# A decoder trunk on one core: six prepared pieces and three parts in the last stage, with more of its products in sevens

## The chip, the core and the metric

The kernel runs on one core of a Trainium2 chip. The metric is the device time of one execution, in microseconds (us). Five engines matter. TensorE (PE) multiplies and transposes, and its weight loads are shown as a row of their own (PEld). VectorE (DVE) does element-wise work. ScalarE (ACT) does casts, copies and functions. GpSimd (POOL) does very little here, and SyncE (SP) issues all DMAs.

## The reference

The reference is a trunk of two layers on 256 tokens of width 2048, all in f32. Each layer has a token mixer (retention in layer 0, a gated short convolution in layer 1) and then a SwiGLU feed-forward part of width 5632. Each half of a layer is normed, scaled and shifted by vectors that come from a conditioning vector, and its result is gated before it is added to the residual. A norm closes the trunk. What the change touches is the feed-forward part of layer 1:

```
h = rms_norm(x, norm2_g[1]) * (1.0 + sc2) + sh2
a, b = jnp.split(h @ ffn_w_in[1], 2, axis=-1)      # (256, 2048) @ (2048, 2 * 5632)
x = x + g2 * ((silu(a) * b) @ ffn_w_out[1])        # (256, 5632) @ (5632, 2048)
return rms_norm(x, final_g)
```

## The kernel before, in words

**Precision in three products.** An f32 matrix is held as two parts, `hi` (the value rounded to the matmul's input type) and `lo` (what is left). A product of two such matrices is three matmuls, hi x hi, hi x lo and lo x hi, added up in a PSUM bank (`thrice`, lines 457 to 462). Weights come from HBM as f32 and are split on the core.

**How weights are prepared.** All weights lie in one array `w_all` in the order of their use, cut into raws of 128 x 2048 (1 MB). `fetch` (line 370) loads one into one of three raw buffers. `prepare` (lines 376 to 406) makes one piece of it: ACT casts it to `hi` (L402), then DVE subtracts to get `lo` (L405). Pieces of 128 x 1024 lie in four places (`PART_BUFS`), each a pair of `hi` and `lo`. `take` (line 410) hands the pieces to PE in order and calls `prepare` so that `ahead_now` pieces beyond the one in use are asked for: two in most of the kernel, three in the last stage (line 1394). A piece's place is free again when PE has read it.

**The order of work.** PE's order is the program's, written out by hand. On DVE and ACT the tile framework's scheduler decides at build time which instruction comes when, by the program's order and given priorities; at run time each engine goes through its queue in that order, and waits on semaphores.

**The last stage.** The feed-forward part of layer 1 works on 44 tiles of 128 of the inner width, in two parts of 20 and 24 tiles (`LAST_TILES`). Four tiles of the first part are made in another way first, while the norm is still being computed (`first_rows`, line 1373). The rest go in *input groups* of four tiles (`last_input`, line 1313): 512 columns of `a` and 512 of `b`, for two halves of 128 tokens each, so four PSUM banks of 128 x 512, summed over the 16 tiles of the width 2048. There are four such groups in the first part and six in the second. After each, DVE and ACT make silu(a) * b, and PE turns the result (eight transposes, L1331), before the third pair of rows in the next group; ACT and DVE then split it into the tiles of `mid`. When a part's input is done, two *output groups* of 1024 columns each (`last_output`, line 1342) multiply its `mid` tiles with the second matrix and add the gated result to the residual `xt` (`gated`, lines 1205 and 1206).

**Pairs and sevens.** The sum of a group runs over pairs of row tiles. With two row tiles, two column blocks of 512 and two halves of tokens, an ordinary pair is eight block products, 24 matmuls of 512 columns, and two pieces of prepared weights. A `Seven` (line 142) does the same by the Strassen-Winograd scheme with seven block products (`sevens`, line 1224): 21 matmuls. It needs sums and differences. Those of the weights are made in `prepare`: DVE makes the differences of 128 x 1024 (L391) and two sums of 128 x 512 (L395, L397), and there are four pieces to split (2, 3, 4 and 5), three of 128 x 1024 and one of 128 x 512. Those of the tokens are made by `tokens_sums_of` (line 1139), for the input once per pair (`made_in_sums`, line 1158), for the output once per pair and part (line 1338). Four of a seven's products go into four extra PSUM banks, and after the last seven of a group `mixed_sums` (line 1237) combines these with one copy on ACT and four operations on DVE, so that with the group's own four banks all eight are in use; DVE adds the plain sums later (L1317, L1365).

`IN_SEVEN` names the pairs done as sevens in an input group (of eight pairs), `OUT_SEVEN` those in the output groups of each part. Which four-wide order the first part's output pairs are taken in is set in `last_out` (line 178), since the last input group's tiles are turned only two pairs into the output. At the end of the last output group, six row tiles are taken column by column, so that one half of the tokens can be finished and stored while PE works on the other (`stored`, line 1249).

Of the kernel before, what the change touches and what calls it, by code (L numbers as in the profile page):

```python
# [17 lines left out]
P = 128  # L18
# [19 lines left out]
LEAD = 6  # L38
ROOTS_AT, SPREAD_AT = 1, 3
TAIL_ROWS = 6  # L40
IN_SEVEN, OUT_SEVEN, TURNS_AT, BESIDE_CB, BESIDE_SUMS = (3, 4, 6), ((2, 4, 6), (2, 4, 6)), 2, 40, 48
LAST_TILES = 20, 24
STORE_AT, LOAD_AT = 0, 2
LEAD_RET, LEAD_CONV, LEAD_FFN = 6, 4, 2
AHEAD = 2
# [2 lines left out]
MOD_PRIO = -300  # L48
STEPS = (8, 8, 20)
RAW_BUFS = 3  # L50
PART_BUFS = 4
LEFT, ENDS, EARLIER = 8, 2, 120

Q0, K0, V0, G0 = 0, HEADS * DK, 2 * HEADS * DK, 2 * HEADS * DK + HEADS * DV
# [112 lines left out]
def last_in():  # L167

    n, rows = LAST_TILES[0], [(i, [2 * i, 2 * i + 1]) for i in range(KT // 2)]
    cols = [part * DFF + j * P for j in range(n - 4, n) for part in range(2)]
    firsts = [Group(cols[:LEAD])] + [Group([c]) for c in cols[LEAD:]]
    fours = [[*range(0, n - 4, 4)], [*range(n, FT, 4)]]
    return firsts, [[in_pairs([j * P, DFF + j * P], rows, IN_SEVEN) for j in js] for js in fours]


def last_out(part):

    first, n = part * LAST_TILES[0], LAST_TILES[part]  # L180
    order = list(range(n // 2))
    if not part:
        a, b = order[-2:]
        order = order[:5] + [a, order[6], b, order[5], order[7]]
    rows = [(i, [first + 2 * i, first + 2 * i + 1]) for i in order]
    out = []
    for c in range(0, D, 2 * DV):
        cols, rest = [c, c + DV], 0
        if part and c + 2 * DV == D:
            rest = TAIL_ROWS // 2  # L190
        out.append(in_pairs(cols, rows[: len(rows) - rest], OUT_SEVEN[part]))
        if rest:
            out[-1] += [Group([col], DV, ks=[k for _, r in rows[-rest:] for k in r]) for col in cols]
    return out


LAST_FIRSTS, LAST_IN = last_in()
LAST_OUT = [last_out(part) for part in range(2)]


def in_use_order():

    for g in RET_SPANS:
        yield "ret_w_in", 0, g
    for n, h in enumerate(HEAD_ORDER):
        qkg, v = RET_HEADS[h]
        for g in qkg[:2] + [v] + qkg[2:]:
            yield "ret_w_in", 0, g
        if n % (HEADS // 2) == HEADS // 2 - 1:
            for g in RET_OUT[n // (HEADS // 2)]:  # L210
                yield "ret_w_out", 0, g
    for layer in range(DEPTH):
        if layer == 1:
            for g in CONV_IN:
                yield "conv_w_in", 0, g
            for g in CONV_OUT:
                yield "conv_w_out", 0, g
        for part in range(2):
            ins, outs = FFN_IN[part], FFN_OUT[part]
            if layer == DEPTH - 1:  # L220
                ins, outs = sum(LAST_IN[part], [] if part else LAST_FIRSTS), sum(LAST_OUT[part], [])
# [35 lines left out]
def trunk(ctx: ExitStack, tc: tile.TileContext, x_in, c_in, pos_in, w_mod, cols_in, gain_in, tab_in, w_all, out):  # L257
# [8 lines left out]
    def name(s):  # L266
        serial[0] += 1
        return f"{s}_{serial[0]}"
# [107 lines left out]
    def prepare(between=None):  # L376
        if prepared[0] == len(pieces):
            return
        _, piece = pieces[prepared[0]]
        prepared[0] += 1  # L380
        if piece in (0, 2):
            if not fetched:
                fetch()
            raws[:] = [fetched.pop(0)]
            while first <= units[0] < early and len(fetched) < RAW_BUFS - 1 and n_fetched[0] < w_all.shape[0]:
                fetch()
        whole = raws[0]
        b = [whole[:, i : i + DV] for i in range(0, CHUNK, DV)]
        raw = whole[:, :HALF] if piece in (0, 4) else whole[:, HALF:]
        if piece == 2:  # L390
            nc.vector.tensor_tensor(differences, whole[:, DV : 3 * DV], whole[:, : 2 * DV], op=ALU.subtract)  # L391
        elif piece == 3:
            raw = differences
        elif piece == 4:
            nc.vector.tensor_tensor(b[1], b[2], differences[:, :DV], op=ALU.subtract)  # L395
        elif piece == 5:
            nc.vector.tensor_tensor(b[3], b[3], b[1], op=ALU.subtract)  # L397
            raw = b[3]
        width = raw.shape[1]
        hi = wpool.tile([P, HALF], F32R, tag="hi", name=name("hi"))[:, :width]  # L400
        lo = wpool.tile([P, HALF], F32R, tag="lo", name=name("lo"))[:, :width]
        nc.scalar.copy(hi, raw)  # L402
        if between:
            between()
        nc.vector.tensor_tensor(lo, raw, hi.bitcast(F32), op=ALU.subtract)  # L405
        ready.append((hi, lo, width))

    prepared, ahead_now = [0], [AHEAD]

    def take(group, k, col, width=P):  # L410

# [778 lines left out]
    def spread():  # L1190
        whole = gate_row.rearrange("a b -> (a b)").unsqueeze(0)
        for i in range(2):
            o = slice(i * D // 2, (i + 1) * D // 2)
            nc.sync.dma_start(flat[i], whole[:, o].broadcast_to([P, D // 2]))
    total = mpool.tile([P, 2, 4], F32, tag="total", name="total")
    sums_of = mpool.tile([P, 2], F32, tag="sums", name="sums")

    def flat_bank():
        return bank().rearrange("p a b -> p (a b)")
# [69 lines left out]
    def gathered(groups, act, base, sums, beside=None, mixed=None):  # L1269

        ours = {(t, j): flat_bank() for t in range(2) for j in range(2)}
        banks, n = [], len(sums)
        for i, g in enumerate(groups):
            if beside:
                beside(i)
            if i == TURNS_AT and waiting:
                waiting.pop(0)()
            if isinstance(g, Seven):
                n -= 1
                banks = banks or [flat_bank() for _ in range(4)]  # L1280
                of = sums[(g.ks[0] - base) // 2]
                sevens(g, act, base, of, ours, banks, n == len(sums) - 1, n == 0)
                if not n:
                    extra = mixed_sums(banks)
                    if mixed:
                        mixed(extra)
                continue
            if len(g.cols) == 1:
                tail = TAIL_ROWS if g is groups[-1] else 0
                late, j = [], g.cols[0] // DV % 2  # L1290
                for k in g.ks:
                    weights = take(g, k, *g.items[0])
                    rows = (act[k - base], False, k == g.ks[-1])
                    if tail:
                        late.append((*weights, *rows))
                    else:
                        by_token([ours[t, j] for t in range(2)], *weights, *rows)
                    paced(g.n)
                for t in range(2):
                    for args in late:  # L1300
                        by_token([ours[t, j] for t in range(2)], *args, halves=[t])
                    added(t, g.cols[0] // DV, ours[t, j], True)
                    if tail:
                        stored(t)
                continue
            for k in g.ks:
                for j, item in enumerate(g.items):
# [33 lines left out]

    def last_output(part, c, groups, act, base):

        final = part and c

        def beside(i):
            if not part and not c and i == STORE_AT:
                gate_stored()
            if not part and not c and i == LOAD_AT:
                spread()  # L1350
            if part and not c and i == LOAD_AT:
# [13 lines left out]
            nc.vector.tensor_tensor(extra[t, j], pt, extra[t, j], op=ALU.add)  # L1365
        for (t, j), v in extra.items():
            gated(t, c + j, v, MOD_PRIO)
            if part:
# [16 lines left out]
            for turn_of in turns[4 * (i - 1) : 4 * i] if i else ():  # L1385
                turn_of()

    for part in range(2):
        n = LAST_TILES[part] // 2
        mid = mids(LAST_TILES[part]) if part else first_mid  # L1390
        if not part:
            first_rows(mid[-2:])
            made_in_sums()
            ahead_now[0] = AHEAD + 1
        for i, groups in enumerate(LAST_IN[part]):
            due = OUT_SEVEN[part]
            seven = [tokens_sums[due.index(q)] if q in due else None for q in (2 * i, 2 * i + 1)]
            last_input(groups, mid[2 * i : 2 * i + 2], seven)
        act = [mid[k // 2][:, k % 2] for k in range(2 * n)]
        for c, groups in enumerate(LAST_OUT[part]):  # L1400
            last_output(part, 2 * c, groups, act, part * LAST_TILES[0])
    assert not todo


# [34 lines left out]
```

## Time and profile before

| what | value |
|---|---|
| runs, us | 2594.22, 2595.54, 2592.18; median 2594.22 |
| profiled execution, us | 2593.25 |
| its span, us | 2591.5 |
| mean granted TensorE clock | 0.998 |
| DVE busy over the span | 2197.4 us, 85% |
| HBM traffic | 689.56 MB, mean 266 GB/s |

The page of a profile gives each engine's busy time as a share of the span. A view by stretches gives the same for any window, and the number of instructions in it after an x. A view by line groups instructions: line, engine, operation, output and input tiles with their shapes and count, then the busy time and the mean duration in ns of one, then the engine's idle time just before them and what ended it. The timeline has one row per instruction, or per run of equal ones: start, duration, engine, line, tiles, count, and in brackets the idle time before it. The view of waits has the waiting engine and tile, what it waited for, and the total in us, the count and the longest. Matmuls are pipelined, so their shown durations overlap, and what one costs is read from the distance between starts.

### The profile page before, as it was taken

The page shows a single profiled execution, that of the slowest core. Times are in us where ns is not written, and L with a number is a line of the kernel's source. Part 1 is how long each engine was busy: PE and PEld are TensorE (multiplying, and loading weights), DVE is VectorE, ACT ScalarE, POOL GpSimd, SP SyncE. Part 2 cuts the span into 40 slices and gives each one's busy share as a digit, 9 for nine tenths or more (in the row PEclk, how much of TensorE's full clock was granted, in tenths as well). Part 3 has the DMA queues.
Part 4 walks back from the last instruction along what each step waited for, and adds up shares of the span by engine and source line. Part 5 has one row for each costly group of instructions (what it writes and reads, how often), then busy time and mean ns, then how long its engine had stood idle before and what let it go on. Part 6 is the DMA issues. An engine that isn't in the chain of part 4 may idle for free.

```text
span 2591.5 us, 36408 instructions
## 1 busy us (share of the span) xinstructions
PE 2563.3 (99%) x14181; PEld 2236.3 (86%) x14181; DVE 2197.4 (85%) x2762; ACT 1306.0 (50%) x1792; POOL 125.9 (5%) x232
## 2 busy tenths in 40 slices
PE   7999999999999999999999999999999999999998
PEld 6898889888889888888888898888998888888887
DVE  7988978787698887777778889988989998999978
ACT  5544543444456545334444454444565554556554
POOL 0000000110000000100001001000000000000001
PEclk9999999999999999999999999999999999999999
DMA  9975768767676888777877768877845565555654
GB/s 398 388 293 209 268 243 306 300 248 277 251 282 246 330 323 307 301 296 298 298 294 283 298 237 313 330 297 277 308 165 210 188 223 205 180 210 187 222 208 147
DMA packets 96688, 689.56 MB, mean 266 GB/s; under 512 B 10737, under 2 KB 12161, under 8 KB 13441
## 3 DMA queue, kind: packets, MB, share of 16 engines
q1 hardware_dynamic: 96514, 687.23, 71.3%
q8 instruction: 111, 1.82, 0.3%
q14 instruction: 63, 0.52, 0.1%
HBM read 685.08 MB, written 2.11 MB: 265 GB/s over the span
## 4 chain that ended last, share of the span: by engine, by line
PE 94%; DVE 3%; DMA 2%; issue 1%; ACT 1%; ACTq 0%; POOLq 0%; POOL 0%; DVEq 0%
PE bank L447 30%; PE bank L450 16%; PE bank L461 12%; PE bank L460 12%; PE bank L462 12%; PE bank L495 2%; PE bank L496 2%; PE bank L494 2%; PE bank L627 1%; PE bank L629 1%; PE bank L628 1%; DVE raw L755 1%; DMA raw<-w_all 1%; DVE lo L405 1%; PE bank L983 1%
## 5 line engine op out<-in xcount | busy, mean ns | idle before, releaser
L402 ACT CAST hi<-raw 128x1024 fp32r<-128x1024 f32 (+1 forms) x954 | 978.9, 1033 | 1015.8 <-PE bank L447 346.4
L405 DVE TENSOR_TENSOR lo<-raw,hi 128x1024 fp32r<-128x1024 f32 (+1 forms) x954 | 1133.9, 1197 | 322.6 <-ACT hi L402 317.3
L447 PE MATMUL bank<-h,hi 128*128 128x512 f32 x2016 | 699.3, 390 | 0.0
L450 PE MATMUL bank<-h,lo 128*128 128x256 f32 x2016 | 568.5, 282 | 0.0
L447 PEld LDWEIGHTS bank<-h,hi 128*128 128x128 f32 x2016 | 378.4, 188 | 79.2
L460 PE MATMUL bank<-hi,h 128*128 128x512 f32 x1032 | 405.0, 392 | 2.2 <-DVE rm L739 2.2
L461 PE MATMUL bank<-lo,h 128*128 128x512 f32 x1032 | 404.3, 392 | 0.0
L462 PE MATMUL bank<-hi,h 128*128 128x512 f32 x1032 | 402.7, 390 | 0.0
L450 PEld LDWEIGHTS bank<-h,lo 128*128 128x128 f32 x2016 | 381.0, 189 | 0.1
L318 DVE SCALAR_TENSOR_TENSOR raw<-raw,cb 128x2048 f32<-128x2048 f32 x160 | 365.5, 2284 | 15.7 <-DMA raw<-w_mod 15.3
L447 PE MATMUL bank<-mid,hi 128*128 128x512 f32 x922 | 319.8, 390 | 0.0
L450 PE MATMUL bank<-mid,lo 128*128 128x256 f32 x922 | 260.1, 282 | 0.4 <-DVE lo L405 0.4
L460 PEld LDWEIGHTS bank<-hi,h 128*128 128x128 f32 x1032 | 194.4, 188 | 40.7 <-DVE rm L739 2.8
L462 PEld LDWEIGHTS bank<-hi,h 128*128 128x128 f32 x1032 | 194.2, 188 | 40.8
L461 PEld LDWEIGHTS bank<-lo,h 128*128 128x128 f32 x1032 | 194.5, 188 | 40.4 <-DVE lo L405 3.3
L447 PEld LDWEIGHTS bank<-mid,hi 128*128 128x128 f32 x922 | 173.1, 188 | 36.2
L450 PEld LDWEIGHTS bank<-mid,lo 128*128 128x128 f32 x922 | 174.2, 189 | 0.7 <-DVE lo L405 0.7
L447 PE MATMUL bank<-rm,hi 128*128 128x512 f32 x496 | 172.5, 390 | 0.0
L496 PE MATMUL bank<-h,lo 128*128 128x256 f32 x512 | 146.4, 286 | 4.6 <-DVE lo L405 4.6
L494 PE MATMUL bank<-h,hi 128*128 128x256 f32 x512 | 146.1, 285 | 3.4 <-ACT h L783 3.4
L495 PE MATMUL bank<-h,hi 128*128 128x256 f32 x512 | 146.1, 285 | 0.7 <-DVE h L784 0.7
L450 PE MATMUL bank<-rm,lo 128*128 128x256 f32 x496 | 139.8, 282 | 0.0
(256 smaller groups left out, 3197.4 us busy)
## 6 DMA issues: line engine op xcount, KB each, us to landing
raw<-w_all SPq DMA_DIRECT2D x456, 1024.0 KB, 4.8
raw<-w_mod SPq DMA_DIRECT2D x192, 1024.0 KB, 5.2
x<-x_in SPq DMA_DIRECT2D x4, 512.0 KB, 5.3
out<-xt SPq DMA_DIRECT2D x4, 512.0 KB, 3.0
decay<-tab_in SPq DMA_DIRECT2D x8, 128.0 KB, 2.4
x<-gate_row SPq DMA_DIRECT2D x2, 512.0 KB, 4.8
last_gain<-gain_in SPq DMA_DIRECT2D x1, 1024.0 KB, 7.2
cols<-cols_in SPq DMA_DIRECT2D x1, 152.0 KB, 8.3
```

Of the source, the lines that this page charges most:

```text
L318: nc.vector.scalar_tensor_tensor(raw, raw, 1.0, cb, op0=ALU.mult, op1=ALU.mult, accum_out=total)
L402: nc.scalar.copy(hi, raw)
L405: nc.vector.tensor_tensor(lo, raw, hi.bitcast(F32), op=ALU.subtract)
L447: nc.tensor.matmul(pt, hi, h, start=fresh and k == g.ks[0], stop=False, skip_group_check=True)
L450: nc.tensor.matmul(pt[:, 1, :], lo, h[:, 0, :], start=False, stop=last and k == g.ks[-1], skip_group_check=True)
L460: nc.tensor.matmul(o, hi, w_hi, start=first, stop=False)
L461: nc.tensor.matmul(o, hi, w_lo, start=False, stop=False)
L462: nc.tensor.matmul(o, lo, w_hi, start=False, stop=last)
L494: nc.tensor.matmul(pt, hi, h[:, 0, :], start=first, stop=False, skip_group_check=True)
L495: nc.tensor.matmul(pt, hi, h[:, 1, :], start=False, stop=False, skip_group_check=True)
L496: nc.tensor.matmul(pt, lo, h[:, 0, :], start=False, stop=last, skip_group_check=True)
L627: nc.tensor.matmul(pt, hi, high, start=k == 0, stop=False, skip_group_check=True)
```

## The change

- The last stage goes in three parts of 12, 16 and 16 tiles instead of two of 20 and 24. There are still ten input groups (two, four and four), but six output groups instead of four.
- Four of the eight pairs of each input group are sevens (3, 4, 5, 6 instead of 3, 4, 6). In the output, two pairs of six are sevens in the first part and three of eight in each of the others; before, three of ten and three of twelve.
- In the last stage two more places for prepared pieces lie in the pool `last`, used by turns with the four of before, and five pieces beyond the one in use are asked for instead of three.
- The two small tiles `total` and `sums_of` move to another pool, and a spacing tile gets smaller.
- `gathered` counts a group's sevens from the group itself.

```diff
-IN_SEVEN, OUT_SEVEN, TURNS_AT, BESIDE_CB, BESIDE_SUMS = (3, 4, 6), ((2, 4, 6), (2, 4, 6)), 2, 40, 48
-LAST_TILES = 20, 24
+IN_SEVEN, OUT_SEVEN, TURNS_AT, BESIDE_CB, BESIDE_SUMS = (3, 4, 5, 6), ((1, 2), (3, 4, 6), (2, 3, 4)), 2, 40, 32
+LAST_TILES = 12, 16, 16
...
-PART_BUFS = 4
+PART_BUFS, MORE_BUFS = 4, 2
...
-    first, n = part * LAST_TILES[0], LAST_TILES[part]
-    order = list(range(n // 2))
+    first = sum(LAST_TILES[:part])
+    order = list(range(LAST_TILES[part] // 2))
     if not part:
-        a, b = order[-2:]
-        order = order[:5] + [a, order[6], b, order[5], order[7]]
+        n = len(order) - 5
+        order = order[:n] + order[-2:] + order[n:-2]
...
-        if part and c + 2 * DV == D:
+        if part == len(LAST_TILES) - 1 and c + 2 * DV == D:
...
-        hi = wpool.tile([P, HALF], F32R, tag="hi", name=name("hi"))[:, :width]
-        lo = wpool.tile([P, HALF], F32R, tag="lo", name=name("lo"))[:, :width]
+        pool, bufs = wpool, PART_BUFS
+        if last_pool and prepared[0] % (PART_BUFS + MORE_BUFS) < MORE_BUFS:
+            pool, bufs = last_pool[0], MORE_BUFS
+        hi = pool.tile([P, HALF], F32R, tag="hi", name=name("hi"), bufs=bufs)[:, :width]
+        lo = pool.tile([P, HALF], F32R, tag="lo", name=name("lo"), bufs=bufs)[:, :width]
...
-    total = mpool.tile([P, 2, 4], F32, tag="total", name="total")
-    sums_of = mpool.tile([P, 2], F32, tag="sums", name="sums")
+    total = work.tile([P, 2, 4], F32, tag="total", name="total", bufs=1)
+    sums_of = work.tile([P, 2], F32, tag="sums", name="sums", bufs=1)
...
-    for part in range(2):
-        n = LAST_TILES[part] // 2
-        mid = mids(LAST_TILES[part]) if part else first_mid
+    for part, tiles in enumerate(LAST_TILES):
+        mid = mids(tiles) if part else first_mid
         if not part:
             first_rows(mid[-2:])
             made_in_sums()
-            ahead_now[0] = AHEAD + 1
+            last_pool.append(mpool)
+            ahead_now[0] = AHEAD + 1 + MORE_BUFS
```

More of the change, by code (lines that the diff above doesn't have):

```diff
@@ L173, in last_in @@
     firsts = [Group(cols[:LEAD])] + [Group([c]) for c in cols[LEAD:]]
-    fours = [[*range(0, n - 4, 4)], [*range(n, FT, 4)]]
+    fours = [[*range(0, n - 4, 4)]]
+    for m in LAST_TILES[1:]:
+        fours.append([*range(n, n + m, 4)])
+        n += m
     return firsts, [[in_pairs([j * P, DFF + j * P], rows, IN_SEVEN) for j in js] for js in fours]
 def last_out(part):
-    first, n = part * LAST_TILES[0], LAST_TILES[part]
-    order = list(range(n // 2))
+    first = sum(LAST_TILES[:part])
+    order = list(range(LAST_TILES[part] // 2))
     if not part:
-        a, b = order[-2:]
-        order = order[:5] + [a, order[6], b, order[5], order[7]]
+        n = len(order) - 5
+        order = order[:n] + order[-2:] + order[n:-2]
     rows = [(i, [first + 2 * i, first + 2 * i + 1]) for i in order]
@@ L197 @@
 LAST_FIRSTS, LAST_IN = last_in()
-LAST_OUT = [last_out(part) for part in range(2)]
+LAST_OUT = [last_out(part) for part in range(len(LAST_TILES))]
 def in_use_order():
@@ L217, in in_use_order @@
                 yield "conv_w_out", 0, g
-        for part in range(2):
-            ins, outs = FFN_IN[part], FFN_OUT[part]
-            if layer == DEPTH - 1:
-                ins, outs = sum(LAST_IN[part], [] if part else LAST_FIRSTS), sum(LAST_OUT[part], [])
+        parts = list(zip(FFN_IN, FFN_OUT))
+        if layer == DEPTH - 1:
+            parts = [(sum(ins, [] if i else LAST_FIRSTS), sum(outs, [])) for i, (ins, outs) in enumerate(zip(LAST_IN, LAST_OUT))]
+        for ins, outs in parts:
             for g in ins:
@@ L406, in prepare @@
         ready.append((hi, lo, width))
-    prepared, ahead_now = [0], [AHEAD]
+    prepared, ahead_now, last_pool = [0], [AHEAD], []
     def take(group, k, col, width=P):
@@ L1271, in gathered @@
         ours = {(t, j): flat_bank() for t in range(2) for j in range(2)}
-        banks, n = [], len(sums)
+        banks, n = [], sum(isinstance(g, Seven) for g in groups)
+        left = n
         for i, g in enumerate(groups):
@@ L1278, in gathered @@
             if isinstance(g, Seven):
-                n -= 1
+                left -= 1
                 banks = banks or [flat_bank() for _ in range(4)]
                 of = sums[(g.ks[0] - base) // 2]
-                sevens(g, act, base, of, ours, banks, n == len(sums) - 1, n == 0)
-                if not n:
+                sevens(g, act, base, of, ours, banks, left == n - 1, left == 0)
+                if not left:
                     extra = mixed_sums(banks)
@@ L1342, in last_output @@
     def last_output(part, c, groups, act, base):
-        final = part and c
+        last = part == len(LAST_TILES) - 1
+        final = last and c
         def beside(i):
@@ L1350, in beside @@
                 spread()
-            if part and not c and i == LOAD_AT:
+            if last and not c and i == LOAD_AT:
                 last_gain = hpool.tile([P, D], F32, tag="h", name="last_gain")
@@ L1367, in last_output @@
             gated(t, c + j, v, MOD_PRIO)
-            if part:
+            if last:
                 xs, n = at(xt[t], c + j), c + j
@@ L1386, in first_rows @@
                 turn_of()
-    for part in range(2):
-        n = LAST_TILES[part] // 2
-        mid = mids(LAST_TILES[part]) if part else first_mid
+    for part, tiles in enumerate(LAST_TILES):
+        mid = mids(tiles) if part else first_mid
         if not part:
@@ L1398, in trunk @@
             last_input(groups, mid[2 * i : 2 * i + 2], seven)
-        act = [mid[k // 2][:, k % 2] for k in range(2 * n)]
+        act = [mid[k // 2][:, k % 2] for k in range(tiles)]
         for c, groups in enumerate(LAST_OUT[part]):
-            last_output(part, 2 * c, groups, act, part * LAST_TILES[0])
+            last_output(part, 2 * c, groups, act, sum(LAST_TILES[:part]))
     assert not todo
```

## The prediction

> **What bounds the kernel now.** I read the page first, then the table of stretches for the last stage alone, then the timelines of TensorE (PE) and VectorE (DVE) in it, then the waits, then the groups by line with shapes kept apart.
>
> ```profile
> span 2591.5 us, 36408 instructions
> ...
> PE 2563.3 (99%) x14181; PEld 2236.3 (86%) x14181; DVE 2197.4 (85%) x2762; ACT 1306.0 (50%) x1792; POOL 125.9 (5%) x232
> ```
>
> The page says only that PE is always busy and that DVE is second. The change touches one stage, so the share that counts is that stage's. It runs from the first product of the first paired group (1923.8) to the last matmul (2582.4):
>
> ```profile
> core 0: us, PE busy (x) PEld busy (x) DVE busy (x) ACT busy (x) POOL busy (x), PEclk, DMA share, GB/s
> 1923.80:2582.40 658.60, 658.06 (x2934) 542.18 (x2932) 593.70 (x712) 366.70 (x433) 7.46 (x7) 1.00 0.55 195
> 2574.10:2582.40 8.30, 8.30 (x38) 6.67 (x36) 5.96 (x11) 2.79 (x8) 2.08 (x5) 1.00 0.00 0
> 2311.30:2353.90 42.60, 42.60 (x192) 35.09 (x191) 39.98 (x51) 25.34 (x31) 0.00 (x0) 1.00 0.55 198
> ```
>
> In this stage DVE is busy 593.7 of 658.6 us, 90%: 64.9 us are free. In one input group (the last row) it is 39.98 of 42.60, so 2.6 us are free. ACT (366.7) and the DMA engines (0.55) have room.
>
> Is PE at its peak, or only shown as busy? Its timeline gives the pitch:
>
> ```profile
> 1923.82 0.48 PE L460 MATMUL bank<-hi,h 128*128 128x512 f32 x1
> ...
> 1940.26 0.39 PE L460 MATMUL bank<-hi,sum 128*128 128x512 f32 x1
> ...
> 1949.78 0.39 PE L460 MATMUL bank<-hi,h 128*128 128x512 f32 x1
> ...
> 1992.39 0.39 PE L460 MATMUL bank<-hi,h 128*128 128x512 f32 x1
> ...
> 2035.00 0.39 PE L460 MATMUL bank<-hi,h 128*128 128x512 f32 x1
> ...
> 2582.17 0.39 PE L462 MATMUL bank<-hi,mid 128*128 128x512 f32 x1
> ```
>
> Two sevens, 42 matmuls, lie between 1940.26 and 1949.78: 9.52 / 42 = 0.2267 us each. An ordinary pair is 24 matmuls, 5.44 us; a seven is 21, 4.76 us. A whole input group takes 2035.00 - 1992.39 = 42.61 us; five pairs and three sevens are 183 matmuls, 41.48 us, and the eight transposes take the other 1.13. Over the stage, ten input groups (1830 matmuls), the output of the first part (2 x (10 x 24 - 9) = 462) and of the second (2 x (12 x 24 - 9) = 558) are 2850 matmuls, 646.1 us; with 11.3 of transposes 657.4, against 658.6. So PE sets the stage, and all its waiting comes to little over 1 us.
>
> The waits of the stage show how DVE and ACT stand to it:
>
> ```profile
> ACT hi L402 <- PE bank L462: 215.6, 224, 1.9
> DVE lo L405 <- ACT hi L402: 57.1, 80, 1.5
> ...
> PEld bank L461 <- DVE lo L405: 4.6, 12, 1.0
> ```
>
> ACT waits for PE to free a prepared piece's place, and DVE waits for ACT: preparation is ahead, held by the four places. PE's weight loads waited for DVE only 4.6 us, most of it hidden.
>
> **The change, part by part.** *PE.* Sevens in the input matrix go from 10 groups x 3 = 30 to 10 x 4 = 40 (still ten groups: 2 + 4 + 4). In the output matrix they go from 2 x (3 + 3) = 12 to 2 x (2 + 3 + 3) = 16. That is 14 more, each three matmuls less: 14 x 3 x 0.2267 = 9.5 us. Transposes stay at 80. PE would need 658.6 - 9.5 = 649.1 us.
>
> *DVE.* These rows carry its prices; first the groups, then their pitch where they run back to back:
>
> ```profile
> L405 DVE TENSOR_TENSOR lo<-raw,hi 128x1024 fp32r<-128x1024 f32 x245 | 296.4, 1220 | 52.3 <-ACT hi L402 49.3
> ...
> L391 DVE TENSOR_TENSOR x<-raw 128x1024 f32<-128x1024 f32 x42 | 51.1, 1217 | 0.3 <-DMA raw<-w_all 0.3
> L397 DVE TENSOR_TENSOR raw<-raw 128x512 f32<-128x512 f32 x42 | 29.0, 690 | 1.0
> L405 DVE TENSOR_TENSOR lo<-raw,hi 128x512 fp32r<-128x512 f32 x42 | 28.8, 686 | 6.7 <-ACT hi L402 6.5
> L395 DVE TENSOR_TENSOR raw<-raw,x 128x512 f32<-128x512 f32 x42 | 28.7, 683 | 0.0
> ...
> L1168 DVE TENSOR_TENSOR u<-h 128x256 f32<-128x256 f32 x4 | 1.7, 418 | 0.0
> ```
>
> ```profile
> 2327.74 0.68 DVE L1317 TENSOR_TENSOR x<-bank,x 128x512 f32<-128x512 f32 x1
> 2328.34 0.68 DVE L1317 TENSOR_TENSOR u<-bank,u 128x512 f32<-128x512 f32 x1
> ...
> 2342.09 0.28 DVE L512 TENSOR_TENSOR mid<-u,mid 128x128 fp32r<-128x128 f32 x1
> 2342.29 0.28 DVE L1146 TENSOR_TENSOR u<-u,u 128x128 f32<-128x128 f32 x1
> ...
> 2343.63 0.55 DVE L512 TENSOR_TENSOR in_cb<-u,in_cb 128x384 fp32r<-128x384 f32 x1
> 2344.10 1.82 DVE L405 TENSOR_TENSOR lo<-raw,hi 128x1024 fp32r<-128x1024 f32 x2
> ...
> 2352.69 3.49 DVE L405 TENSOR_TENSOR lo<-raw,hi 128x1024 fp32r<-128x1024 f32 x3
> 2356.10 1.22 DVE L405 TENSOR_TENSOR lo<-x,hi 128x1024 fp32r<-128x1024 f32 x1
> 2357.23 0.68 DVE L395 TENSOR_TENSOR raw<-raw,x 128x512 f32<-128x512 f32 x1
> 2357.95 0.69 DVE L397 TENSOR_TENSOR raw<-raw 128x512 f32<-128x512 f32 x1
> ```
>
> A 1024-wide operation lasts 1.22 us, but three in a row take 3.49: (3.49 - 1.22) / 2 = 1.135 from start to start. A 512-wide one starts 0.60 after the last (2327.74 to 2328.34), or 0.72 behind one whose result it needs (L395 to L397). A 128-wide one takes 0.20, the 384-wide one 0.47. So the next instruction starts 0.085 us before the one ahead has ended, and each gap that closes frees 0.085 more than the idle time shows.
>
> An ordinary pair costs DVE two 1024-wide `lo`: 2.27 us. A seven costs one difference and three `lo` of 1024 (4.54), one `lo` of 512 (0.60), and L395 and L397 (1.32): 6.46. So a seven gives PE 0.68 us and takes 4.19 from DVE; fourteen take 58.7. The third part brings two more output groups, each with the four sums of the mixed products, four additions of the plain ones and eight operations with gate and residual: 2 x 16 x 0.60 = 19.2. Two more output pairs need sums of tokens (five 128-wide and one 384-wide, 1.47): 2.9. One more input pair needs them (two of 256 at 0.42 from L1168's mean, eight of 0.20): 2.4. Sum: 83.2 us.
>
> One price is weighed here. The Trainium skill (VectorE: DVE Perf Modes, section "Side-by-side: where the cycles go") gives an instruction its elements plus 8 and some 150 cycles at 0.96 GHz, which would be about 1.23 us for 1024 and 0.70 for 512; as an estimate, the 28 wide and 74 half-wide instructions added would then cost 34.5 + 51.7, with the small ones about 92 us, and the forecast would be some 15 us later. The trace agrees with 1.22 as a duration, but the 3.49 for three shows that the next one does not wait for it, so the pitch stands.
>
> *What DVE has for it.* 64.9 us idle and 80 x 0.085 = 6.8 from the gaps (the 80 waits above): 71.7. The need is 83.2. Even with no idle moment DVE is 83.2 - 71.7 = 11.5 us short, so DVE becomes the bound and PE's 9.5 us are lost in waiting. By one input group the same: DVE's 39.98, less 0.4 for five gaps, plus 4.19 is 43.8 us, against PE's 42.61 - 0.68 = 41.93.
>
> *Idle time that stays.* In the last 8.30 us DVE is idle for 2.3: the weights are all prepared and the end hangs on the last products. That stays: 13.8. Inside, an input group now has 2.34 us of gaps (2.6 less rounding at its edges); over ten groups 23.4. All stand behind casts that waited for a place, so six places should close most; but four sevens run one after the other now (pairs 3 to 6), each a chain of DVE, ACT and DVE again. Bounds for what stays: nothing and 23.4. I take 6, a quarter, since the waits above name PE's places for 215.6 us. Sum: 13.8 + 6 = 19.8.
>
> *Edits at nothing.* Six places instead of four fit in what four tiles less of `mid` leave, and hold at most two pieces more ahead: once, at the start, 2 x 1.135 = 2.3 us, only in the low bound, since DVE is not idle there. `total` and the sums only change their pool. ACT gets 14 x 1.5 casts of about 1 us, 21 on 366.7, and stays the third engine. The weights are the same megabytes in the same loads. Sums of tokens for pair 2 of the first part are needed two pairs after their transposes (10.2 us) instead of four: about 3 us of DVE work, covered unless DVE is behind, and then it is in the sum already.
>
> The profiled run took 2593.25 us, 1.75 more than its span; 2593.25 + 19.8 = 2613.1. The median of the runs shown is 0.97 above the profiled one: **2614**.
>
> **The rivals.** *DVE keeps up, faster.* If the gaps are only want of places, six places close them, PE never waits, and the gain is the whole 9.5: 2594.2 - 9.5 = 2584.7. It decides where DVE's work in an input group falls below 41.93 us; for it speaks that every gap is behind a place, against it 43.8. The Trainium skill (Perfetto Trace Analysis, section "Optimization Strategy") says that the same gap repeated can mean too few buffers; the trace agrees with the 215.6 us of ACT behind PE's places, and by that rule the outcome is this rival's.
>
> *About the same.* DVE's work is dearer than PE's saving, but some prices are lower than the pitch says; 83.2 would have to be 65, a fifth less, for 2594 to 2596.
>
> *Much slower: the chains stay.* The two further places do not help (held by pieces that wait for each other, or DVE's order puts a wait for PE's bank ahead of the piece that PE wants): all 23.4 of gaps remain. 13.8 + 23.4 = 37.2: 2631.4. For it speaks the line of four sevens, 19.0 us of PE against 25.8 of DVE; against it that today's casts wait for PE rather than for DVE. It would also be the time if the places did not come into use at all.
>
> **How the numbers follow.** Forecast 0.65, the chains stay 0.20, DVE keeps up 0.08, the same 0.07. Own range of the forecast: 11.5 (the tail's 2.3 met by the lead) to 13.8 + 16, so 2605.7 to 2624. The range reaches up to the chains, 2632, and down by 5% of DVE's sum (4.2), to 2601. A measurement of this kernel can tell about 0.2%, 5.2 us, from no change. Faster by over that: 0.08; within: 0.07; slower: 0.85.
>
> **What would show it.** Right: in the last stage PE's matmul count falls by 42 but the stage is some 20 us longer; DVE is busy about 98% there; the waits of PE's weight loads on DVE `lo` grow from 4.6 to 20 us or more, mostly in pairs 3 to 6 of the input groups; ACT's waits for PE's places shrink from 215.6 to well under half. An input group takes about 44 us rather than 42.61. Wrong: input groups of 41.9 us with PE at its pitch throughout (DVE's prices or my count are off), or DVE idle as now while PE waits (the chains).

## The result, and the profile after

The changed kernel takes 2623.14 us (median of 4, 2621.87 to 2624.13), the kernel before beside it 2593.20 (median of 4): 1.0117 times as long, 95% interval 1.0105 to 1.013, or 29.9 us. The forecast was 2614 and slower, with a range from 2601 to 2632. The granted clock was the same in both (0.998 and 0.997), so it has no part in this. Lines of the changed file stand three to eight lower: the cast to `hi` is L408, the subtraction for `lo` L411, the difference L394, and the sums L398 and L400.

The page of the changed kernel, to be read against that of before:

```profile
span 2622.3 us, 36476 instructions
## 1 busy us (share of the span) xinstructions
PE 2563.2 (98%) x14139; PEld 2228.5 (85%) x14139; DVE 2273.2 (87%) x2886; ACT 1321.7 (50%) x1832; POOL 121.3 (5%) x232
...
PE 75%; DVE 17%; DMA 3%; issue 3%; ACT 2%; POOL 0%; ACTq 0%; DVEq 0%; SPq 0%
```

PE has 42 matmuls less, as counted, and is shown busy as long as before: a busy PE here is a PE that holds an instruction. The last line, the chain that ended last, tells more. Before, DVE had 3% of it, and now it has 17%; the line of before:

```profile
PE 94%; DVE 3%; DMA 2%; issue 1%; ACT 1%; ACTq 0%; POOLq 0%; POOL 0%; DVEq 0%
```

The table of stretches cuts the last stage at the first product with `mid` and the first one with `h`, so its rows are in turn the input and the output groups of each part; the last row is what lies behind the last matmul. The kernel before first, then the changed one:

```profile
1923.82:2093.46 169.64, 169.64 (x760) 139.57 (x759) 157.20 (x202) 99.91 (x125) 0.00 (x0) 1.00 0.55 193
2093.46:2200.06 106.60, 106.06 (x472) 87.55 (x471) 91.66 (x107) 55.61 (x62) 0.00 (x0) 1.00 0.59 212
2200.06:2454.79 254.73, 254.73 (x1140) 209.75 (x1138) 236.35 (x279) 146.02 (x167) 0.00 (x0) 1.00 0.55 196
2454.79:2582.40 127.61, 127.61 (x567) 105.29 (x565) 108.46 (x127) 65.14 (x79) 7.46 (x7) 1.00 0.51 181
2582.40:2591.50 9.10, 0.16 (x1) 0.00 (x0) 3.08 (x6) 2.67 (x5) 0.55 (x1) 0.68 0.58 230
```

```profile
1924.17:2013.33 89.16, 84.41 (x373) 68.03 (x371) 87.64 (x129) 52.85 (x76) 0.00 (x0) 1.00 0.48 177
2013.33:2076.97 63.64, 63.64 (x286) 52.52 (x284) 62.43 (x77) 36.57 (x44) 0.00 (x0) 1.00 0.64 233
2076.97:2258.30 181.33, 170.95 (x745) 138.06 (x745) 174.78 (x212) 99.22 (x117) 0.00 (x0) 0.99 0.49 179
2258.30:2342.17 83.87, 83.87 (x375) 69.52 (x374) 80.65 (x96) 47.89 (x55) 0.00 (x0) 1.00 0.58 215
2342.17:2520.26 178.09, 170.04 (x746) 136.62 (x744) 174.31 (x215) 100.06 (x120) 0.00 (x0) 1.00 0.50 183
2520.26:2608.38 88.12, 85.18 (x375) 69.02 (x373) 86.69 (x106) 43.91 (x57) 1.77 (x3) 1.00 0.45 168
2608.38:2622.30 13.92, 0.16 (x1) 0.00 (x0) 5.73 (x12) 4.51 (x10) 2.18 (x5) 0.67 0.38 151
```

The ten input groups took 169.64 + 254.73 = 424.4 us and now take 89.16 + 181.33 + 178.09 = 448.6, though PE's own work in them is 6.8 us less. The output groups took 234.2 and now take 235.6. So of the 30.8 us by which the span grew, 24.2 came in the input groups, 1.4 in the output, 4.8 behind the last matmul (9.1 before, 13.9 now), and 0.35 lies ahead of the stage. DVE, the third busy figure of a row, fills every input row to 96% or more.

The waits of the stage in the changed kernel:

```profile
ACT hi L408 <- PE bank L468: 110.1, 75, 4.7
ACT hi L408 <- DVE raw L398: 59.0, 32, 4.0
ACT hi L408 <- DVE x L394: 48.1, 21, 3.5
ACT hi L408 <- DMA raw<-w_all: 38.4, 31, 3.1
PEld bank L467 <- DVE lo L411: 26.8, 25, 1.8
PE bank L467 <- DVE lo L411: 17.3, 19, 1.3
DVE lo L411 <- ACT hi L408: 13.5, 24, 1.6
...
PEld bank L466 <- DVE x L1250: 6.1, 3, 3.5
PE bank L466 <- DVE x L1250: 4.8, 3, 3.1
```

DVE's wait for ACT's casts has gone from 57.1 to 13.5 us, and ACT now waits for DVE (59.0 and 48.1, were 33.2 and 4.5) about as much as for PE's places (110.1, was 215.6). PE's weight loads wait for `lo`, 26.8 us where it was 4.6. The order of who waits for whom has turned round. One wait is new: ACT's casts wait 38.4 us for the loads of raw weights, for which they did not wait before. The raw buffers are still three, and in both kernels the DMA queue waits for DVE's subtraction (L405, now L411) ahead of 119 of the stage's loads.

### The profile page after: what moved, and what is told of

The parts are those of the page before. It is cut to its first block, busy times and chain, and to the rows that moved or that the text cites. A ratio compares the mean times of both kernels' runs of the same rounds, so it can differ in the third digit from the quotient of the medians.

```text
span 2622.3 us, 36476 instructions
## 1 busy us (share of the span) xinstructions
PE 2563.2 (98%) x14139; PEld 2228.5 (85%) x14139; DVE 2273.2 (87%) x2886; ACT 1321.7 (50%) x1832; POOL 121.3 (5%) x232
## 4 chain that ended last, share of the span: by engine, by line
PE 75%; DVE 17%; DMA 3%; issue 3%; ACT 2%; POOL 0%; ACTq 0%; DVEq 0%; SPq 0%
PE bank L453 28%; PE bank L456 15%; DVE lo L411 8%; PE bank L467 7%; PE bank L468 7%; PE bank L466 7%; DMA raw<-w_all 3%; PE bank L502 2%; PE bank L501 2%; PE bank L500 2%; DVE x L394 2%; PE bank L633 1%; PE bank L635 1%; PE bank L634 1%; ACT hi L408 1%
## 5 line engine op out<-in xcount | busy, mean ns | idle before, releaser
L408 ACT CAST hi<-raw 128x1024 fp32r<-128x1024 f32 (+1 forms) x968 | 975.2, 1026 | 957.5 <-PE bank L453 296.7
L411 DVE TENSOR_TENSOR lo<-raw,hi 128x1024 fp32r<-128x1024 f32 (+1 forms) x968 | 1137.9, 1192 | 267.5 <-ACT hi L408 264.0
L467 PE MATMUL bank<-lo,h 128*128 128x512 f32 x992 | 390.4, 394 | 15.3 <-DVE lo L411 15.2
L466 PE MATMUL bank<-hi,h 128*128 128x512 f32 x992 | 391.5, 395 | 9.9 <-DVE x L1250 4.8
L468 PE MATMUL bank<-hi,h 128*128 128x512 f32 x992 | 387.8, 391 | 0.0
L467 PEld LDWEIGHTS bank<-lo,h 128*128 128x128 f32 x992 | 187.4, 189 | 57.5 <-DVE lo L411 22.6
L466 PEld LDWEIGHTS bank<-hi,h 128*128 128x128 f32 x992 | 187.2, 189 | 51.7 <-DVE x L1250 6.1
L468 PEld LDWEIGHTS bank<-hi,h 128*128 128x128 f32 x992 | 187.1, 189 | 39.0
```

The source lines that it names most:

```text
L466: nc.tensor.matmul(o, hi, w_hi, start=first, stop=False)
L467: nc.tensor.matmul(o, hi, w_lo, start=False, stop=False)
L468: nc.tensor.matmul(o, lo, w_hi, start=False, stop=last)
```

## The experiments

Three theories were tested. *Work*: VectorE's sum of work sets the stage, either over the whole stage or within each input group. *Row of sevens*: the chain from DVE to ACT and back in four sevens one after the other stalls, and places would bridge it. *Parts*: the third part and its end cost the time. Each ratio below is to the kernel before, timed beside it on the same chip; the chips differ from one experiment to another, so two experiments are compared best by their ratios. Where a diff changes one name of a line that sets several, only that name is shown.

**Three parts, old sevens in the input.**

```diff
-IN_SEVEN = (3, 4, 5, 6)
+IN_SEVEN = (3, 4, 6)
```

> Three parts and six places as changed, output sevens as changed, but three sevens per input group as before. Theory of work (VectorE's sum of work sets the last stage): VectorE gets 4 more sevens x 4.19 + two output groups 19.2 + sums of tokens 2.9 = 38.9 us more, under the 71.7 us it has free; TensorE needs 4 x 0.68 = 2.7 us less, so 2588 to 2596. Rival of the parts (the third part's two output groups and its end are what costs): over 2605. Rival of the row of sevens (four in a row stall the chain): as the theory of work, since no four stand in a row.

2591.35 us, 0.9995 (0.9985 to 1.0004): no change. The third part, its two output groups, four more output sevens and six places cost nothing together. So with six places the ten additional input sevens cost 2623 - 2591 = 32 us, and the rival of the parts falls as it was put (over 2605). With four places both come out differently, as a run below shows.

**Two parts, four sevens in the input.** This is the same addition by itself, on the kernel before.

```diff
-IN_SEVEN = (3, 4, 6)
+IN_SEVEN = (3, 4, 5, 6)
```

> The kernel before with four sevens per input group (pairs 3 to 6) and nothing else: two parts, four places. Theory of work taken over the whole stage: 10 x 4.19 + 2.4 = 44.3 us of VectorE's 71.7, TensorE 6.8 less, 2586 to 2594. Theory of work taken group by group (43.8 us of VectorE per input group, which the output groups can't make good): 10 x 1.2 longer, about 2605. Rival of the row of sevens: over 2612.

2607.10 us, 1.0052 (1.0037 to 1.0067). The stage, cut into input and output groups of each part as above:

```profile
1921.04:2097.70 176.66, 172.98 (x748) 135.78 (x746) 173.48 (x231) 107.07 (x137) 0.00 (x0) 1.00 0.50 185
2097.70:2203.45 105.75, 105.75 (x472) 87.63 (x471) 92.06 (x108) 55.70 (x63) 0.00 (x0) 1.00 0.59 213
2203.45:2468.10 264.65, 259.62 (x1122) 204.06 (x1120) 258.08 (x308) 155.72 (x180) 0.00 (x0) 1.00 0.51 189
2468.10:2595.72 127.62, 127.62 (x567) 105.32 (x565) 108.84 (x128) 64.71 (x79) 7.48 (x7) 1.00 0.49 181
```

DVE is idle for 42.2 us of 674.7, and still the stage is 16 us longer than the 658.6 of before. Of this idle time 9.8 us lie in the input groups and 32.5 in the output groups, where the additional work isn't: the account holds group by group, not over the whole stage. The expected 2605 of that reading was met to 2 us.

**Four places.**

```diff
-PART_BUFS, MORE_BUFS = 4, 2
+PART_BUFS, MORE_BUFS = 4, 0
```

> The changed kernel with four places and three pieces asked for ahead, as before. Theory of work: VectorE is short of time whatever it has in store, so within some 12 us of the changed kernel, 2618 to 2635. Rival of the row of sevens (the chain from VectorE to ScalarE and back is what stalls, and places are what bridges it): over 2640.

2618.20 us, 1.0095 (1.008 to 1.011). Where DVE is short of time, the two places bring nothing; the kernel is rather 5 us faster without them. That speaks against the row of sevens. One moment of the changed kernel shows a price of running far ahead. At 2384.84 the second input group of the third part begins, and PE needs banks that DVE is still to free with the merging of the group before (L1249 to L1252). DVE, then PE, then ACT:

```profile
2383.33 1.23 DVE L411 TENSOR_TENSOR lo<-raw,hi 128x1024 fp32r<-128x1024 f32 x1 [0.43 <-ACT hi L408]
2384.48 0.68 DVE L1249 TENSOR_TENSOR u<-bank,x 128x512 f32<-128x512 f32 x1
...
2386.21 0.68 DVE L1250 TENSOR_TENSOR x<-bank,u 128x512 f32<-128x512 f32 x1
...
2388.54 0.68 DVE L1252 TENSOR_TENSOR u<-bank,u 128x512 f32<-128x512 f32 x1
```

```profile
2386.95 0.50 PE L466 MATMUL bank<-hi,h 128*128 128x512 f32 x1 [0.58 <-DVE x L1250]
...
2389.28 0.50 PE L466 MATMUL bank<-hi,h 128*128 128x512 f32 x1 [1.37 <-DVE u L1252]
```

```profile
2382.25 1.05 ACT L408 CAST hi<-raw 128x1024 fp32r<-128x1024 f32 x1 [3.09 <-DMA raw<-w_all]
2383.21 0.58 ACT L1248 COPY x<-bank 128x512 f32<-128x512 f32 x1
```

The copy that begins the merging (L1248) stands in ACT's queue behind a cast for a later piece, and that cast waited 3.09 us for its load. The merging on DVE comes behind the `lo` of that same piece, with two more `lo` in between. Over the whole stage PE's matmuls wait 8.7 us behind DVE's operations on banks with six places and 1.4 with four. In return its weight loads wait less for `lo` (26.8 against 42.8). The two stages are nearly equal, 684.2 and 682.9. Of the 6.2 us between the two profiled spans, 1.4 lie in the stage, 2.3 behind the last matmul, and 2.5 ahead of the stage, where the edit changes nothing: the stage begins between 1921.0 and 1925.9 us in the runs of this document. So in this pair 3.7 us fall where the places are in use.

**Three parts, old sevens, four places.**

```diff
-IN_SEVEN = (3, 4, 5, 6)
+IN_SEVEN = (3, 4, 6)
-PART_BUFS, MORE_BUFS = 4, 2
+PART_BUFS, MORE_BUFS = 4, 0
```

> Three parts and three sevens per input group as in the run of that name, but four places instead of six. If the two places are worth something only where VectorE has time to get ahead, TensorE's weight loads wait 5 to 8 us more in the last stage than with six, and the whole takes 2595 to 2600. If the places are worth nothing anywhere, as between the changed kernel and the same with four, 2590 to 2593.

2601.58 us, 1.0034 (1.0022 to 1.0046), against 0.9995 with six. Here the two places are worth 10 us: DVE has time to get ahead, and PE's weight loads wait 11.8 us for `lo` with four places and 1.0 with six. So the places pay where DVE has time in sum and lacks it only in a burst. The time is a little over the 2595 to 2600 that was expected.

Read with the runs above, this one also shows that no part of the change has a price of its own. With four places the third part and its output sevens cost 9 us (2601.58 against 2592.55 beside it), which six places give back. With four places the ten additional input sevens cost 2618.20 - 2601.58 = 16.6 us, about as in two parts (15.3), and not 32. What the kernels with three parts and four input sevens have in common is a stage of 683 to 684 us, with four places or six. What the places shorten is the stage with three: 663.1 us with four, 653.5 with six.

**The difference on GpSimd.**

```diff
-nc.vector.tensor_tensor(differences, whole[:, DV : 3 * DV], whole[:, : 2 * DV], op=ALU.subtract)
+nc.gpsimd.tensor_tensor(differences, whole[:, DV : 3 * DV], whole[:, : 2 * DV], op=ALU.subtract)
```

> The changed kernel with the differences of 128 x 1024 that a seven needs made on GpSimd instead of VectorE. Theory of work: 56 x 1.135 = 63.6 us leave VectorE, 83.2 - 63.6 = 19.6 of its 71.7 us are needed, TensorE sets the stage again: 2584 to 2595. Rival of the row of sevens: the chain gets longer by a slower engine, so 2623 or over.

2662.15 us, 1.0268 (1.025 to 1.0285): far outside the range of the theory of work, and inside that of its rival. The work left DVE, but two things came back. The changed kernel's groups on DVE first, then this kernel's, and its GpSimd group:

```profile
L400 DVE TENSOR_TENSOR raw<-raw 128x512 f32<-128x512 f32 x56 | 38.8, 692 | 1.0
L398 DVE TENSOR_TENSOR raw<-raw,x 128x512 f32<-128x512 f32 x56 | 38.7, 691 | 0.0
...
L1324 DVE TENSOR_TENSOR x<-bank,x 128x512 f32<-128x512 f32 x20 | 13.7, 685 | 0.8 <-PE bank L468 0.8
```

```profile
L400 DVE TENSOR_TENSOR raw<-raw 128x512 f32<-128x512 f32 x56 | 62.5, 1116 | 0.6
...
L398 DVE TENSOR_TENSOR raw<-raw,x 128x512 f32<-128x512 f32 x56 | 38.3, 683 | 43.7 <-POOL x L394 43.7
L1329 DVE TENSOR_TENSOR x<-x,u 128x512 f32<-128x512 f32 x20 | 21.5, 1082 | 0.7 <-ACT x L1328 0.7
L1324 DVE TENSOR_TENSOR x<-bank,x 128x512 f32<-128x512 f32 x20 | 13.6, 682 | 0.0
```

```profile
L394 POOL TENSOR_TENSOR x<-raw 128x1024 f32<-128x1024 f32 x56 | 174.8, 3121 | 568.2 <-DMA raw<-w_all 275.7 <-DVE lo L411 165.9 <-DVE raw L398 67.4
```

A difference takes 3.12 us on GpSimd, and DVE stands still for 43.7 us behind it. And DVE's own operations get longer: L400 goes from 692 to 1116 ns on average, with nothing changed in it. The average hides two kinds: 45 of the 56 stay at about 0.69 us, and 11 are longer, up to 2.89. The Trainium skill (SBUF — State Buffer, section "SBUF: two separate sides") says that a pair of ports is shared by GpSimd and a VectorE operation with two SBUF inputs, and that whichever starts first holds it for the whole instruction. The trace agrees. L400 reads two SBUF tiles: its 11 longer ones all began after a difference on GpSimd had begun and ended 0.55 us behind it, and 17 others that began before the difference beside them stayed short. L1324 reads a PSUM bank, lies beside a difference 25 times of 40 and stays at 0.68 us. L398 reads two SBUF tiles too and stays at 0.68, but it waits for GpSimd's result and so never runs beside it.

DVE is busy for 666.7 us of the stage, as in the changed kernel, and idle for 60.2. So the run exchanged one shortage of DVE for another and added a wait for a slower engine, which is what the rival said of this run. It decides nothing between the two theories. A cleaner way to take the work away follows.

**Without the difference.** The same subtraction is left out, so that the sevens compute with a tile that isn't theirs; all else stays.

```diff
-nc.vector.tensor_tensor(differences, whole[:, DV : 3 * DV], whole[:, : 2 * DV], op=ALU.subtract)
+pass
```

> The changed kernel without the subtraction that makes a seven's difference of 128 x 1024; the tile keeps what lay in it, so the sevens compute with other numbers. Everything else, matmuls, casts, places and order, stays. Theory of work: 56 x 1.135 = 63.6 us leave VectorE, which has more than enough time then; TensorE sets the stage at some 649 us and the whole takes 2582 to 2590. Group by group the same, 43.8 - 4.5 = 39.3 us against 41.93. Rival of the row of sevens (ScalarE's and VectorE's chain through the casts, not the sum of work): over 2605.

2582.78 us, 0.9959 (0.9945 to 0.9973):

```profile
1923.93:2569.97 646.04, 646.04 (x2892) 535.24 (x2890) 608.42 (x777) 382.52 (x468) 1.80 (x4) 1.00 0.54 199
```

With the matmuls, casts, parts and places of the changed kernel and 56 VectorE instructions less, PE runs the stage in 646.0 us, 12.5 less than before, and no row of four sevens stalls anything. PE's 9.5 us were there to be had; DVE's work took them. The other 3 us came from small waits of the kernel before: what the starts of its matmuls lie apart beyond 0.2267 us adds up to 3.7 us in the stage, in pieces of about 0.1 that the view of waits leaves out, and to 1.2 here. One reservation: the run takes away a link of the chain as well as work, since ACT's cast of a difference no longer waits for it (48.1 us in the changed kernel). By itself it doesn't tell the two apart.

**The same work without a seven more.** The kernel before, with each difference computed two or three times over:

```diff
             nc.vector.tensor_tensor(differences, whole[:, DV : 3 * DV], whole[:, : 2 * DV], op=ALU.subtract)
+            nc.vector.tensor_tensor(differences, whole[:, DV : 3 * DV], whole[:, : 2 * DV], op=ALU.subtract)
```

> The kernel before, each seven's difference of 128 x 1024 made twice over: 42 x 1.135 = 47.7 us more of VectorE's work, no matmul more or less, no other wait. Theory of work, whole stage: 47.7 is under the 71.7 us free, so no change, 2590 to 2596. Theory of work, group by group: three more per input group, 3.4 us against some 2.6 to 3 us free, so 4 to 12 us longer, 2596 to 2604. Rival of the row of sevens (it is four sevens in a row that stall, not the work): no change.

> The kernel before, each seven's difference made three times: 95.3 us more of VectorE's work, 6.8 per input group. Theory of work, whole stage: 95.3 - 71.7 = 23.6 longer, plus what stays idle, 2616 to 2625. Theory of work, group by group: 6.8 - 3 = 3.8 per input group, 38, and little from the output groups, 2625 to 2640. Rival of the row of sevens: under 2600, as no row got longer.

Two: 2599.82 us, 1.0031 (1.0019 to 1.0043). Three: 2646.49 us, 1.0215 (1.0199 to 1.0231). So 47.7 us of added work cost 7.9, and 95.3 cost 54.6: the price sets in about where the free time of the input groups is used up (30.8 us in the kernel before, against 30 x 1.135 = 34.1 added there), and between the two points each microsecond of DVE's work costs about one, (54.6 - 7.9) / 47.7 = 0.98. The stage with three:

```profile
1921.75:2632.28 710.53, 675.59 (x2934) 541.55 (x2932) 686.74 (x793) 360.37 (x430) 5.08 (x6) 1.00 0.48 181
```

DVE is busy for 686.7 us of 710.5; 23.8 us stay idle even so. The group-by-group expectation for two was met; for three it fell short (2625 to 2640): the input groups grew by 43.1 us where 38 was said, and the output groups by 8.9 where it was little.

**Sevens apart.** Pairs 2, 3, 5, 6 in the place of 3, 4, 5, 6 in the changed kernel:

```diff
-IN_SEVEN = (3, 4, 5, 6)
+IN_SEVEN = (2, 3, 5, 6)
```

> The changed kernel with the four sevens of an input group at pairs 2, 3, 5 and 6 instead of 3, 4, 5 and 6. Theory of work: the sum is the same, within 6 us of the changed kernel, 2617 to 2629. Rival of the row of sevens: two rows of two with an ordinary pair between them need far less in store, under 2608.

2621.15 us, 1.0112 (1.0098 to 1.0126), the same as the changed kernel. By the rival of the row of sevens it should have been under 2608, so that rival falls.

**The end: priority of the last gate.** Two runs, in the changed kernel and in the one with three parts and the old input sevens:

```diff
-            gated(t, c + j, v, MOD_PRIO)
+            gated(t, c + j, v, 0 if last else MOD_PRIO)
```

> The changed kernel with the gate and residual of the last part's first output group at ordinary priority instead of the low one. If the 4.8 us more behind the last matmul come from those operations being put off to the end, the stretch behind the last matmul goes from 13.9 back to about 9 us, and the time to 2617 to 2620. If that stretch comes from VectorE's backlog itself, no change, 2621 to 2625.

> Three parts, six places, three sevens per input group, and the gate and residual of the last part's first output group at ordinary priority. TensorE's stage without the put-off end: 2591.4 - 4.8 = 2586.5, 2585 to 2588, faster than the kernel before by 0.2%. If the end is VectorE's backlog, no change against the same kernel with the low priority, 2590 to 2593.

2622.72 us (1.0119, 1.0105 to 1.0132) and 2590.89 (0.9997, 0.9989 to 1.0006). Neither time moved. The stretch behind the last matmul did: 11.5 us in the first where it was 13.9, and 11.6 in the second where it was 13.7. So the low priority makes about half of the 4.8 us. In the second the stage got 2.2 us longer in return; in the first it stayed (684.1), and the median of the runs does not show the gain.

**A longer last part.**

```diff
-IN_SEVEN, OUT_SEVEN = (3, 4, 5, 6), ((1, 2), (3, 4, 6), (2, 3, 4))
-LAST_TILES = 12, 16, 16
-PART_BUFS, MORE_BUFS = 4, 2
+IN_SEVEN, OUT_SEVEN = (3, 4, 6), ((1, 2), (2, 3), (2, 3, 5))
+LAST_TILES = 12, 12, 20
+PART_BUFS, MORE_BUFS = 4, 0
```

> Three sevens per input group, three parts of 12, 12 and 20 tiles, output sevens at pairs 1, 2; 2, 3; and 2, 3, 5; four places. If the 4.8 us more behind the last matmul are VectorE's backlog of merging, because only three ordinary pairs follow the last seven in a part of 16 tiles, then with four pairs behind it the stretch goes down to 9 to 11 us; TensorE has two sevens more than before, 1.4 us less: 2587 to 2591 in all. If the third part itself costs the end, the stretch stays at 13 to 14.

2596.57 us, 1.0017 (1.0008 to 1.0026), so the time was missed: four places seem to cost here what they cost in the run with three parts (PE's weight loads wait 10.4 us for `lo`, 11.8 there). The stretch behind the last matmul is 10.4 us, as the backlog of merging would have it. But it is 11.6 in the two runs with four places and a last part of 16 tiles, and 10.9 without the differences, so places move it, and so do the differences of the last output groups. The ten input sevens do not: 13.9 with them and 13.7 without at six places, 11.6 and 11.6 at four. That the end is DVE's backlog of merging and gates fits all of these; how much of it each cause has is open.

None of these kernels that compute the reference is faster than the one before; three parts with three sevens and six places equal it.

## Why the prediction was right

**The mechanism was right.** DVE had 71.7 us to give, a seven costs it 4.19 and brings PE 0.68, and the stage became DVE's. This rests on the trace, where DVE is busy for 97.4% of the stage, and on experiments from both sides: DVE's work added without a seven makes the kernel before slower (three differences), and DVE's work taken away from the changed kernel gives PE's gain (no difference). Both edits also change the chain through ACT's casts; that the row of four sevens isn't the cause rests on the runs with sevens apart and with four places.

**PE's saving, 9.5 us.** Right: 42 matmuls less, and it was had in full when DVE had time. In the changed kernel it was lost in waits, as said. That all of PE's waiting before came to little over 1 us was a misreading: it was 3.7, counted by starts.

**DVE's added work, 83.2 us.** A little high. DVE was busy 666.5 us of the stage against 593.7, 72.8 more. DVE's waits for casts went from 80 to 24; closing 56 gaps at 0.085 hides 4.8, and 2.65 were put off behind the last matmul: 80.2.

**Idle time that stays, 8.3 us.** This is the mis-sized term. DVE was idle for 684.21 - 666.51 = 17.7 us of the stage, and the run with three differences, where DVE is shorter of time still, shows 23.8. The 6 us taken for the inside of the groups were a quarter of the bound, and the input groups alone kept 1.5 + 6.6 + 3.8 = 11.9. The tail's 2.3, which were to stay, went: DVE is busy for all of the last 8.30 us of the stage.

```profile
2600.08:2608.38 8.30, 6.96 (x31) 5.23 (x29) 8.30 (x13) 1.34 (x4) 1.08 (x2) 1.00 0.00 1
```

By the terms of the sum: DVE's busy time grew 3.6 less than forecast, its idle time is 9.4 more, and 19.8 - 3.6 + 9.4 gives the 25.6 us that the stage grew.

**The end.** The sum had no term for the stretch behind the last matmul, which grew by 4.8 us. With only three ordinary pairs behind the last seven, DVE still had work to do when PE was done (5.73 us, 3.08 before); the run with four such pairs and four places has 10.4 us behind the last matmul, against 11.6. 25.6 + 4.8 + 0.35 ahead of the stage make the span's 30.8.

**By the whole stage or by the group.** The forecast gave both accounts and went by the whole stage. Here they nearly agree, since the output groups became full too (62.43 of 63.64, 80.65 of 83.87). That is chance: with four input sevens in two parts, DVE had 42 us idle and the kernel was slower all the same. The account by group, 43.8 us against PE's 41.93, was the sounder one. The changed kernel's input groups took 44.9 on average: 43.7 of DVE's work, as said, and 1.2 idle, which neither account had.

**The rivals.** *DVE keeps up* gave 2584.7; the kernel without the differences took 2582.8. So the rival's point of decision, DVE's work in an input group below PE's 41.93 us, was rightly placed: DVE is busy for 43.7 us of a group in the changed kernel and for 39.2 without the differences. The Trainium skill's rule on too few buffers (Perfetto Trace Analysis, section "Optimization Strategy"), on which it leaned, is borne out where DVE has time in sum (10 us between three parts with four and with six places) and not where it lacks it. *The chains stay* fell as a mechanism: fewer places and sevens apart did not move the time as that rival needs. But the number gives it no clear defeat: 2623 lies about midway between 2614 and its 2631, and DVE's idle time, 17.7 us, between the forecast's 8.3 and its 25.7. What the idle time that is left consists of, the trace shows in part. Of DVE's 13.5 us behind casts, 6.0 follow a cast that had waited for one of PE's places itself, or through one ahead of it on ACT (50.9 of 57.1 before), 2.4 one that had waited for a load, and 1.4 one that had waited for a sum of DVE's own.

**What the profile was to show.** An input group of some 44 us, DVE at 97.4% where 98% was said, and PE's weight loads behind `lo` for 26.8 us where 20 or more was said: as forecast. Of the 26.8, 21.8 lie in pairs 4 to 6 of the input groups, as was also said. ACT's waits for places went to 110.1 of 215.6, about half, not well under half. PE's waits behind DVE's operations on banks (8.7 us), and ACT's for loads (38.4), were not forecast: the loads were put at nothing, as the same megabytes.

## What to carry to other kernels

A trick that saves the first engine's work by giving some to the second is priced by the ratio of the two, and by the second engine's free time in the very stretch where the trick is used: here 0.68 us of PE for 4.19 of DVE, with under 3 us free per group. Buffers turn idle time from one moment into time at another; here they helped where the second engine had enough time in sum (10 us) and did nothing where it had not. So what a part of a change costs depends on the parts that are in already, and one run without it doesn't give its price. The engine that filled up kept 2 to 3% idle here, and left work undone at the very end: a forecast by sums needs a term for both.

## What the runs showed of the hardware that was not expected

GpSimd beside VectorE: a difference of 128 x 1024 in f32 took 3.12 us on GpSimd against a pitch of 1.135 on VectorE. VectorE's 128 x 512 operations with two SBUF inputs stayed at 0.69 us beside it where they began first (17 on line L400); where GpSimd began first they lasted until 0.55 us behind its end, up to 2.89 (11 on L400). Those with a PSUM input stayed at 0.68 beside it in either case.
